# More pairs with seven products in the four output blocks of a hybrid decoder layer, with two input mixes made in the heads' stage

## The chip, the cores and the metric

The kernel runs on one core of a Trainium2 chip, as one program. The metric is the device time of one execution in microseconds (us). A core has five engines with a list of instructions each: TensorE (PE; its weight loads are shown apart, as PEld), VectorE (DVE), ScalarE (ACT), GpSimd (POOL) and SyncE (SP). Each engine goes through its list in order; semaphores make it wait for another engine or a DMA.

## The reference

One decoder layer for 256 tokens of 2048 channels, in float32. The normalised input goes through one wide projection; from it come a latent attention with 16 heads and a gated short convolution. The part that matters here stands behind both:

```python
y_mla = jnp.einsum('bse,ed->bsd', attn, w_o_mla)
...
y_conv = jnp.einsum('bse,ed->bsd', b_gate * conv * jax.nn.silu(z_conv), w_o_conv)
merged = jax.nn.sigmoid(g_mla) * y_mla + jax.nn.sigmoid(g_conv) * y_conv
out = jnp.einsum('bsd,de->bse', merged, w_out)
x = x + _rmsnorm(out, post_norm_g)
```

`g_mla` and `g_conv` are two slices of the wide projection. So four products of 256 x 2048 by 2048 x 2048 are computed in a row: two gates from the normalised input `h`, the attention branch, the convolution branch. The kernel calls them n = 0, 1, 2, 3.

## The kernel before

**Precision.** A float32 product is made of three matmuls: each operand is split into a high and a low half, and high x high, high x low and low x high are added in a bank of PSUM (`product`). For the weights ACT copies the high half (`whi`) and DVE subtracts it to get the low half (`wlo`); both happen in `split_act`. The activations stand split in `x_both` (high in the first 256 columns, low behind them).

**Weights.** All weights are one list of units, `plan`, of 1 MB each (128 x 2048). SP loads them into a ring of three (`raw`); `take(i)` makes sure that unit i is split, and the units behind it are loaded and split ahead. `whi` and `wlo` are rings of five buffers of 1024 columns. A unit is two buffers of each; ACT waits for PE to free the one that it writes.

**Stages.** First come the latents, then 16 heads (`for h in range(H)`), where the matmuls of the wide projection fill in around the attention. Small blocks are transposed on the way: DVE transposes 32 x 32 squares, POOL sends the block to DRAM and brings it back (`turned`: `far`, then `come`). Then come the four products n = 0 to 3, each in two blocks c = 0, 1 of 1024 output columns, and last `w_out` (the name `out`) and the norm. One block adds up eight pairs: pair k covers input features 256 k to 256 k + 255, as a 2 x 2 of blocks of 128 tokens by 128 features, against a 2 x 2 of weight blocks of 128 x 512. A pair is one unit of weights.

**Two kinds of pair.** A plain pair makes the eight products of a 2 x 2 by a 2 x 2, 24 matmuls. A quick pair makes seven (Winograd's form of Strassen's product), 21 matmuls. For that, `split_seven` (L218) forms sums of weight blocks on DVE (`ts`, L224) and splits them too (`th`, `tl`), and `mixed` (L1004) forms differences of input blocks on DVE (`xr` the whole input, `xm` the four differences) and splits them into `mix`. With seven products a block needs eight banks: p1, q5, q6, q7 and p2, q3, q4, d22. `first_sums` combines the first four into the outputs behind the last quick pair of the block; `last_sums` adds the other four at its end.

**Which pairs are quick.** `FAST = (0, 3, 5)` for the two gates (n = 0, 1; in block (0, 0) only 0 and 3), in `fast_block` (L1029). The branches n = 2, 3 have plain pairs only, in `plain_block` (L1077), with four banks a block. In block (0, 0) the order of pairs is 1, 2, 4, 0, 6, 3, 5, 7, and the three mixes are made inside that block, ahead of the second, fourth and sixth pair. The first quick pair there, pair 0, begins with p1, which needs no mix; q5 (from `mix`, `th` and `tl`), q7 and q6 follow, then p2, q3, q4.

**What sets the order.** PE's matmuls are kept in program order. The other engines' instructions are ordered by a scheduler from the program's order and its estimates, unless `keep_in_program_order` pins them. Rings (`tile_pool` with a tag and a number of buffers) decide when an operation may write.

**What the attention block turns into.** While (1, 1) and (2, 0) run, `split_group` splits the attention's output into `x_both`; while (2, 0) and (2, 1) run, the convolution's into `cv_first` and `x_both`. A branch's result multiplies the gate (L1131, L1137) and is added up (L1138); for the last product it is transposed by `turned` and split again (`features`).

Of the kernel before, what the change touches and what calls it, by code (L numbers as in the profile page):

```python
# [11 lines left out]
F32 = mybir.dt.float32  # L12
# [6 lines left out]
P = 128  # L19
S = 256  # L20
# [64 lines left out]
def tile_layer(ctx: ExitStack, tc: tile.TileContext, xw, w0, xb, x, pos, pvec, post_g, wc, wz, wcv, wkr, wqk, wqr, wv, cwr, wd, wo, out):  # L85
# [57 lines left out]
    fast = {(n, c): FAST if n < 2 else () for n in range(4) for c in range(2)}  # L143
    fast[0, 0] = FAST[:2]
    u_d, seven = {}, set()
# [72 lines left out]
    def split_seven(i, t):  # L218
        hi, hi2 = (wpool.tile([P, HALF], F32R, name=f"whi{i}_{j}", tag="whi", bufs=5) for j in range(2))
        lo, lo2 = (wpool.tile([P, HALF], F32R, name=f"wlo{i}_{j}", tag="wlo", bufs=5) for j in range(2))  # L220
# [9 lines left out]
        split_act(hi2[:, :R], lo2[:, :R], t[:, HALF : 3 * R])  # L230
# [4 lines left out]
        return {"b11": b11, "b22": b22, "b21": (hi2[:, :R], lo2[:, :R]), "t1": t1, "t2": t2, "t3": t3, "t4": t4}  # L235
# [86 lines left out]
    x_both = hp.tile([P, KD, 2 * S], F32R, name="x_both")  # L322
    cstack, astack = (main.enter_context(ExitStack()) for _ in range(2))
# [328 lines left out]

    def make(i, j, *more):
        return {"a": group_a, "r": group_r, "v": group_v}[i](j, *more)
# [197 lines left out]
    for h in range(H):  # L852
# [51 lines left out]
        if h == H - 2:  # L904
            score(h + 1)

# [63 lines left out]
    mix = {k: sp.tile([P, 2, 4 * P], F32R, name=f"mix{k}") for k in FAST[::-1]}  # L970
    sums_lo("home")
# [32 lines left out]
    def mixed(k):  # L1004
        tmp = evens(f"xr{k}")
        f = tmp[:, :].rearrange("p (j s) -> p j s", j=2)
        ks = slice(2 * k, 2 * k + 2)
        nc.vector.tensor_tensor(f, x_both[:, ks, :S].bitcast(F32), x_both[:, ks, S:].bitcast(F32), op=ALU.add)
        raw = evens(f"xm{k}")
        a11, a21, a12, a22 = (f[:, j, t * P : (t + 1) * P] for j in range(2) for t in range(2))  # L1010
        m7, m5, m6, m3 = (raw[:, j * P : (j + 1) * P] for j in range(4))
        minus = lambda o, a, b: nc.vector.tensor_tensor(o, a, b, op=ALU.subtract)
        minus(m7, a21, a11)
        minus(m5, a21, a22)
        minus(m6, a11, m5)
        minus(m3, a12, m6)
        split_act(mix[k][:, 0, :], mix[k][:, 1, :], raw[:, :])

    def mix_part(k, j):
        return tuple(mix[k][:, o, j * P : (j + 1) * P] for o in range(2))  # L1020
# [4 lines left out]
    def fast_block(n, c, part, outs, between):  # L1025
        q = {name: bank(f"{name}_{n}{c}") for name in ("p2", "q3", "q4", "d22")}
        q["p1"] = bank(f"p1_{n}{c}", tag="st", bufs=1)
        q["q5"] = bank(f"q5_{n}{c}", tag="o", bufs=1)
        q["q7"], q["q6"] = (bank(f"{name}_{n}{c}", tag="cv", bufs=2) for name in ("q7", "q6"))  # L1029
        order, quick = pair_order[n, c], fast[n, c]  # L1030
        calls = []
# [16 lines left out]
        t_a, t_b = (evens(f"ev{i}_{n}{c}")[:, :] for i in range(2))  # L1048
        (o11, o12), (o21, o22) = outs
        tt = lambda o, a, b, op=ALU.add: nc.vector.tensor_tensor(o, a, b, op=op)  # L1050

        def first_sums():
            nc.scalar.activation(t_a, q["p1"][:, :], AF.Copy)
            tt(t_b, q["q6"][:, :], t_a, ALU.subtract)
            tt(o12, q["q5"][:, :], t_b)
            tt(o21, q["q7"][:, :], t_b)
            tt(o22, q["q5"][:, :], o21)

        def last_sums():
            tt(o11, q["p2"][:, :], t_a)  # L1060
            tt(o12, q["q3"][:, :], o12)
            tt(o21, q["q4"][:, :], o21, ALU.subtract)
            tt(o22, q["d22"][:, :], o22)
# [11 lines left out]
        last_sums()  # L1075

    def plain_block(n, c, part, between):  # L1077
        tags = ("mm",) * 4 if c else ("st", "o", "cv", "cv")
        q = {
            (t, j): bank(f"sq{n}{c}_{t}{j}", tag=tag, bufs={"mm": 4, "cv": 2}.get(tag, 1))  # L1080
            for (t, j), tag in zip(((0, 0), (0, 1), (1, 0), (1, 1)), tags)
        }
        order = pair_order[n, c]
        for at, k in enumerate(order):
            w = take(u_d[n, c, k])
            between(at)
            for (t, j), ps in q.items():
                for i in range(2):
                    b = w({(0, 0): 0, (1, 1): 1, (1, 0): 2, (0, 1): 3}[i, j], R)
                    product(ps[:, :], part(2 * k + i, t), b, at == i == 0, at == PAIRS - 1 and i == 1)  # L1090
        return q
# [6 lines left out]
    for n in range(2):  # L1098
# [4 lines left out]
        for c in range(2):  # L1103

            def between(i):
                if n == c == 0 and i in (1, 3, 5):
                    mixed(FAST[i // 2])
                if n == c == 1 and i in (2, 4, 6):
                    split_group(at_place, at_t, i // 2 - 1)

            outs = [[gate[n][t][:, columns(c, j)] for j in range(2)] for t in range(NT)]
            fast_block(n, c, x_part, outs, between)
# [3 lines left out]
    def between(c, i):  # L1116
# [7 lines left out]
        if (c, i) in ((0, 4), (0, 6), (1, 3), (1, 5)):  # L1124
            split_group(cv_place, cv_t, {(0, 4): 0, (0, 6): 1, (1, 3): 2, (1, 5): 3}[c, i])

    for c in range(2):
        q = plain_block(2, c, x_part, lambda i: between(c, i))
        for (t, j), ps in q.items():
            g = gate[0][t][:, columns(c, j)]  # L1130
            nc.vector.tensor_tensor(g, ps[:, :], g, op=ALU.mult)  # L1131
# [215 lines left out]
```

## Time and profile before

| | us |
|---|---|
| runs: median (lowest to highest) | 1034.54 (1033.6 to 1034.96) |
| the profiled execution | 1034.48 |
| its span, first to last instruction | 1032.7 |
| gate blocks (n = 0, 1), from the first matmul of (0, 0) | 590.2 to 763.6 |
| branch blocks (n = 2, 3) | 763.6 to 937.7 |
| last product and norm | 937.7 to 1032.7 |

The profile is one execution. Its first part has the busy time of each engine and the share of the span; its fourth the chain of work that ended last; its fifth groups of instructions by source line, engine, operation and tile. Every matmul is on line 90 (`matmul`) and every split on L282 (ACT) and L283 (DVE), so groups there are told apart by the tile names. A matmul shows 389 ns from its start to its end, but the next one starts before it ends: busy time and starts are to be read, not the mean. In a timeline a row has the start, the length, the engine, line, operation and tiles, "x2" for two merged instructions, and in brackets the idle time before it and what ended it. A wait put down to "issue" is one for which the profile shows no releaser.

### The profile page before, as it was taken

Reading aid. Unit: us, or ns where it says so; the run is one execution under the profiler, and the core shown is the slowest. Engines: PE = TensorE matmul, PEld = TensorE weight load, DVE = VectorE, ACT = ScalarE, POOL = GpSimd, SP = SyncE. Lnnn points to the kernel's source line nnn. Section 1 sums busy time; section 2 is a strip of 40 time slices with the busy share of each in tenths; the row PEclk is TensorE's granted clock in tenths of the full one; section 3 lists DMA queues with packets and bytes.
Section 4 is the critical chain, followed back from the end, with each engine's and each line's share of the span. In section 5 each row is a group of like instructions: output and inputs, shape, how many; then the busy total and the mean of one; then the engine's idle time right before and its main releaser. Section 6 shows DMA issues by size and latency. Waiting matters only on the chain.

```text
span 1032.7 us, 12827 instructions
## 1 busy us (share of the span) xinstructions
PE 1022.6 (99%) x4651; PEld 851.5 (82%) x4651; DVE 747.4 (72%) x1062; ACT 543.9 (53%) x764; POOL 179.0 (17%) x344
## 2 busy tenths in 40 slices
PE   9999999999999999999999989999999999999998
PEld 7888888888888888888888868888888888888886
DVE  7588777787777777777877798898875554756572
ACT  7665545655456454564555546555654443344451
POOL 4540421104301223112133120000000000214000
PEclk9999999999999999999999989999999999999999
DMA  9775866568665676757676755555555555577852
GB/s 357 276 260 202 279 205 234 213 201 282 218 246 197 220 263 211 273 192 244 229 269 222 260 183 178 226 206 204 204 198 182 193 202 196 197 258 246 344 184 81
DMA packets 44528, 233.26 MB, mean 226 GB/s; under 512 B 7953, under 2 KB 10513, under 8 KB 21553
## 3 DMA queue, kind: packets, MB, share of 16 engines
q1 hardware_dynamic: 32400, 199.67, 54.8%
q0 software_dynamic: 11632, 29.48, 8.8%
q10 hardware_dynamic: 432, 3.29, 0.8%
q8 instruction: 36, 0.59, 0.2%
q14 instruction: 28, 0.22, 0.1%
HBM read 215.66 MB, written 12.58 MB: 221 GB/s over the span
## 4 chain that ended last, share of the span: by engine, by line
PE 97%; DVE 2%; DMA 0%; ACT 0%; issue 0%
PE cv L90 34%; PE sq L90 17%; PE q L90 8%; PE z L90 8%; PE out L90 8%; PE p L90 4%; PE d L90 2%; PE kn L90 2%; PE qa L90 2%; PE qn L90 2%; PE vv L90 2%; PE ckv L90 2%; PE sc L90 1%; PE qr L90 1%; PE o L90 1%; DVE wlo L283 1%
## 5 line engine op out<-in xcount | busy, mean ns | idle before, releaser
L283 DVE TENSOR_TENSOR wlo<-raw,whi 128x1024 fp32r<-128x1024 f32 (+1 forms) x370 | 431.8, 1179 | 202.8 <-ACT whi L282 195.4
L282 ACT ACTIVATE whi<-raw 128x1024 fp32r<-128x1024 f32 (+1 forms) x372 | 373.2, 1021 | 376.0 <-PE cv L90 116.9
L90 PE MATMUL cv<-whi,x_both 128*128 128x512 f32 x1024 | 319.8, 389 | 0.0
L90 PEld LDWEIGHTS cv<-whi,x_both 128*128 128x128 f32 x1024 | 192.3, 188 | 39.4
L90 PE MATMUL cv<-wlo,x_both 128*128 128x512 f32 x512 | 199.6, 390 | 0.0
L90 PE MATMUL sq<-whi,x_both 128*128 128x512 f32 x384 | 118.8, 389 | 0.0
L90 PEld LDWEIGHTS cv<-wlo,x_both 128*128 128x128 f32 x512 | 96.1, 188 | 19.5 <-DVE wlo L283 0.2
L90 PEld LDWEIGHTS sq<-whi,x_both 128*128 128x128 f32 x384 | 72.1, 188 | 15.0
L90 PE MATMUL z<-whi,x_both 128*128 128x512 f32 x256 | 80.0, 389 | 0.0
L90 PE MATMUL out<-whi,x_both 128*128 128x512 f32 x256 | 79.0, 389 | 0.0
L90 PE MATMUL sq<-wlo,x_both 128*128 128x512 f32 x192 | 74.7, 389 | 0.0
L367 POOL DMA_DIRECT2D far<-g x32 | 17.4, 551 | 322.5 <-DVE g L1138 289.9
L367 POOL DMA_DIRECT2D far<-via x64 | 35.2, 556 | 179.2 <-DVE via L359 178.9
L90 PEld LDWEIGHTS out<-whi,x_both 128*128 128x128 f32 x256 | 48.1, 188 | 9.9
L90 PEld LDWEIGHTS z<-whi,x_both 128*128 128x128 f32 x256 | 48.1, 188 | 9.9
L90 PE MATMUL q<-whi,x_both 128*128 128x512 f32 x168 | 55.1, 389 | 0.0
L90 PE MATMUL z<-wlo,x_both 128*128 128x512 f32 x128 | 49.8, 389 | 0.0
L90 PE MATMUL out<-wlo,x_both 128*128 128x512 f32 x128 | 49.8, 389 | 0.0
L90 PE MATMUL p<-whi,x_both 128*128 128x512 f32 x128 | 46.6, 391 | 0.0
L90 PEld LDWEIGHTS sq<-wlo,x_both 128*128 128x128 f32 x192 | 36.0, 188 | 7.4
L367 POOL DMA_DIRECT2D far<-cw x48 | 26.1, 551 | 79.1 <-DVE cw L359 79.1
L90 PE MATMUL sq<-whi,cv_first 128*128 128x512 f32 x128 | 39.7, 389 | 0.0
(253 smaller groups left out, 1433.0 us busy)
## 6 DMA issues: line engine op xcount, KB each, us to landing
raw<-wcv_dram SPq DMA_DIRECT2D x64, 1024.0 KB, 5.9
raw<-wd_dram SPq DMA_DIRECT2D x64, 1024.0 KB, 4.8
raw<-wz_dram SPq DMA_DIRECT2D x16, 1024.0 KB, 4.8
raw<-wo_dram SPq DMA_DIRECT2D x16, 1024.0 KB, 5.0
raw<-wqk_dram SPq DMA_DIRECT2D x8, 1024.0 KB, 6.1
cw<-cwr_dram POOLq DMA_DIRECT2D x24, 256.0 KB, 6.2
raw<-wc_dram SPq DMA_DIRECT2D x4, 1024.0 KB, 10.4
raw<-wv_dram SPq DMA_DIRECT2D x4, 1024.0 KB, 4.8
```

What stands on the lines that cost most here:

```text
L90: return tc.keep_in_program_order(nc.tensor.matmul(*a, **kw))
L282: a = nc.scalar.activation(hi, src, AF.Copy)
L283: b = nc.vector.tensor_tensor(lo, src, hi.bitcast(F32), op=ALU.subtract)
L367: tc.keep_in_program_order(queue.dma_start(out=f[i], in_=m))
```

## The change

Six pairs of the branch blocks become quick: pair 4 in (2, 0), 4 and 6 in (2, 1), 2 and 5 in (3, 0), 2 in (3, 1). `block` replaces `fast_block` and `plain_block`. The pair order of the last three blocks changes so that quick pairs stand late. Where the outputs are not gate tiles (n = 2, 3), the combined sums stand in the ring `ev` and in a tile `more`, and the gate product and the sum read them from there instead of from PSUM. The two groups of four banks change places from block to block.

The mixes of pairs 0 and 3 are made in the heads' stage, at heads 5 and 9, into tiles that exist from the start; pair 5's stays, at the seventh pair of (0, 0), where it is first used in (0, 1). The branches' mixes use the same two tiles again, each made during the block ahead of or at the start of the one that needs it.

A quick unit's single block, b21, gets rings of its own (`ph`, `pl`, 512 columns, two buffers each), where it took half of a wide buffer of `whi` and `wlo`. The space that POOL's DMAs have for descriptors is set to 8192 bytes a partition; the line did not set it before. In `first_sums` two additions change places.

```diff
+    pair_order[2, 1] = [0, 1, 2, 4, 3, 6, 5, 7]
+    pair_order[3, 0] = [0, 1, 3, 4, 2, 6, 5, 7]
+    pair_order[3, 1] = [0, 1, 3, 2, 4, 5, 6, 7]
-    fast = {(n, c): FAST if n < 2 else () for n in range(4) for c in range(2)}
+    fast = {(n, c): FAST for n in range(2) for c in range(2)}
     fast[0, 0] = FAST[:2]
+    fast.update({(2, 0): (4,), (2, 1): (4, 6), (3, 0): (2, 5), (3, 1): (2,)})
...
     def split_seven(i, t):
-        hi, hi2 = (wpool.tile([P, HALF], F32R, name=f"whi{i}_{j}", tag="whi", bufs=5) for j in range(2))
-        lo, lo2 = (wpool.tile([P, HALF], F32R, name=f"wlo{i}_{j}", tag="wlo", bufs=5) for j in range(2))
+        hi, lo = (wpool.tile([P, HALF], F32R, name=f"{o}{i}", tag=o, bufs=5) for o in ("whi", "wlo"))
+        hi2, lo2 = part_hi(f"ph{i}"), part_lo(f"pl{i}")
...
+    def mixed(dst, place, k, rows, raw):
+        xs = [rows(j) for j in range(2)]
+        for j, x in enumerate(xs):
+            area, at = place(2 * k + j)
+            h, l = (area[:, at, o : o + S].bitcast(F32) for o in (0, S))
+            nc.vector.tensor_tensor(x, h, l, op=ALU.add)
+        a11, a21, a12, a22 = (x[:, t * P : (t + 1) * P] for x in xs for t in range(2))
+        m7, m5, m6, m3 = (raw[:, j * P : (j + 1) * P] for j in range(4))
+        minus = lambda o, a, b: nc.vector.tensor_tensor(o, a, b, op=ALU.subtract)
+        minus(m7, a21, a11)
+        minus(m5, a21, a22)
+        minus(m6, a11, m5)
+        minus(m3, a12, m6)
+        split_act(dst[:, 0, :], dst[:, 1, :], raw)
...
+        if h in (HV + 1, 2 * HV + 1):
+            k = FAST[v - 1]
+            mixed(mix[k], lambda k: (x_both, k), k, lambda j: temp("f")[:, :], temp("cw", (P, 512), bufs=2)[:, :])
...
+    def block(n, c, part, mix, between, outs=None):
+        small = [("st", 1), ("o", 1), ("cv", 2), ("cv", 2)]
+        homes = {False: [("mm", 4)] * 4, True: small}
+        sums_at = n < 2 or c == 1
+        q = {}
+        for at, names in ((not sums_at, ("p2", "q3", "q4", "d22")), (sums_at, ("p1", "q5", "q7", "q6"))):
+            for name, (tag, bufs) in zip(names, homes[at]):
+                q[name] = bank(f"{name}_{n}{c}", tag=tag, bufs=bufs)
...
+        if outs is None:
+            more = sp.tile([P, 2 * R], F32, name=f"more_{n}{c}", tag="spare", bufs=1)
+            outs = [[t_a, t_b], [more[:, :R], more[:, R:]]]
...
-                if n == c == 0 and i in (1, 3, 5):
-                    mixed(FAST[i // 2])
+                if n == c == 0 and i == 6:
+                    mixed_in(mix, at_place, FAST[2])
...
+        if (c, i) in ((0, 2), (1, 1)):
+            mixed_in(mix_at, at_place, fast[2, 1][c])
...
-        q = plain_block(2, c, x_part, lambda i: between(c, i))
+        q = block(2, c, x_part, mix_at, lambda i: between(c, i))
...
+        if c == 0 and i in (1, 2):
+            mixed_in(mix_cv, cv_place, fast[3, 0][i - 1])
...
-        q = plain_block(3, c, cv_part, lambda i: features(i - 4) if c and i in (4, 5) else None)
+        q = block(3, c, cv_part, mix_cv, lambda i: between(c, i))
...
-    nc = bacc.Bacc("TRN2", target_bir_lowering=False, num_devices=1)
+    nc = bacc.Bacc("TRN2", target_bir_lowering=False, num_devices=1, dynamic_dma_scratch_size=8192)
```

What the scheduler made of it is shown at two places of DVE's list. A row has the source line, the operation, the tile written and those read, with buffer numbers, and the size. First, the stretch in which DVE prepares pair 0, the first quick pair of block (0, 0). Before, up to its second low half (`tl_1_5676`) and its mix:

```order
L224 TENSOR_TENSOR ts_1_5672<-ts_1_5672,raw_5622 128x512
L1012 TENSOR_TENSOR xm_5634<-xr_5632,xm_5634 128x128
L224 TENSOR_TENSOR ts_0_5758<-raw_5712 128x1024
L283 TENSOR_TENSOR wlo_1024_5719<-raw_5665,whi_1024_5718 128x1024
L1008 TENSOR_TENSOR xr_5722<-x_both 128x512
L283 TENSOR_TENSOR wlo_0_5756<-raw_5712,whi_0_5754 128x1024
L283 TENSOR_TENSOR tl_1_5676<-ts_1_5672,th_1_5674 128x1024
L283 TENSOR_TENSOR mix_5570<-xm_5634,mix_5570 128x512
```

Now, the same pair from its first sum (`ts_0_5686`) to its second low half (`tl_1_5691`):

```order
L228 TENSOR_TENSOR ts_0_5686<-raw_5646 128x1024
L287 TENSOR_TENSOR pl_5685<-raw_5646,ph_5684 128x512
L228 TENSOR_TENSOR ts_1_5687<-ts_0_5686,raw_5646 128x512
L287 TENSOR_TENSOR wlo_0_5730<-raw_5680,whi_0_5729 128x1024
L287 TENSOR_TENSOR wlo_1024_5734<-raw_5680,whi_1024_5733 128x1024
L228 TENSOR_TENSOR ts_1_5687<-ts_1_5687,raw_5646 128x512
L287 TENSOR_TENSOR tl_0_5690<-ts_0_5686,th_0_5688 128x1024
L287 TENSOR_TENSOR pl_5763<-raw_5727,ph_5762 128x512
L287 TENSOR_TENSOR tl_1_5691<-ts_1_5687,th_1_5689 128x1024
```

The operations on `xr`, `xm` and `mix` are gone from this stretch, and so is the next quick pair's first sum (`ts_0_5758`), which stood ahead of the second low half.

Second, the branch block (2, 1) on DVE. Before, at its start, with the gate products of block (2, 0) (`g<-sq`) and plain units only:

```order
L1131 TENSOR_TENSOR g_1_5573<-sq_11_6915,g_1_5573 128x512
L283 TENSOR_TENSOR wlo_1024_7220<-raw_7171,whi_1024_7219 128x1024
L283 TENSOR_TENSOR wlo_0_7250<-raw_7213,whi_0_7249 128x1024
L283 TENSOR_TENSOR wlo_1024_7254<-raw_7213,whi_1024_7253 128x1024
L283 TENSOR_TENSOR wlo_0_7284<-raw_7247,whi_0_7283 128x1024
L283 TENSOR_TENSOR wlo_1024_7288<-raw_7247,whi_1024_7287 128x1024
L283 TENSOR_TENSOR wlo_0_7318<-raw_7281,whi_0_7317 128x1024
L283 TENSOR_TENSOR wlo_1024_7322<-raw_7281,whi_1024_7321 128x1024
L283 TENSOR_TENSOR x_both<-cv_f,x_both 128x4x128 x2
```

Now, up to the second low half (`tl_1_7352`) of pair 4, the fourth pair of that block:

```order
L228 TENSOR_TENSOR ts_1_7348<-ts_0_7347,raw_7297 128x512
L287 TENSOR_TENSOR wlo_1024_7304<-raw_7263,whi_1024_7303 128x1024
L666 TENSOR_TENSOR xm_7308<-xr_7307,xm_7308 128x128
L287 TENSOR_TENSOR tl_0_7351<-ts_0_7347,th_0_7349 128x1024
L287 TENSOR_TENSOR wlo_7344<-raw_7297,whi_7343 128x1024
L228 TENSOR_TENSOR ts_1_7348<-ts_1_7348,raw_7297 128x512
L666 TENSOR_TENSOR xm_7308<-xr_7307,xm_7308 128x128
L287 TENSOR_TENSOR wlo_0_7391<-raw_7341,whi_0_7390 128x1024
L287 TENSOR_TENSOR wlo_1024_7395<-raw_7341,whi_1024_7394 128x1024
L287 TENSOR_TENSOR x_both<-cv_f,x_both 128x4x128 x2
L228 TENSOR_TENSOR ts_0_7429<-raw_7388 128x1024
L287 TENSOR_TENSOR tl_1_7352<-ts_1_7348,th_1_7350 128x1024
```

Behind the two parts of the unit that follows (`wlo_0_7391`, `wlo_1024_7395`), a split of the convolution's output and the first sum of the next quick pair (`ts_0_7429`) DVE comes to `tl_1_7352`.

80 lines of the change are left out of this document (28 added, 52 removed).

## The prediction

> **What bounds the kernel now.** The profile's page comes first: the span, the busy time of TensorE (PE), and the chain of work that ended last.
>
> ```profile
> span 1032.7 us, 12827 instructions
> PE 1022.6 (99%) x4651; PEld 851.5 (82%) x4651; DVE 747.4 (72%) x1062; ACT 543.9 (53%) x764; POOL 179.0 (17%) x344
> PE 97%; DVE 2%; DMA 0%; ACT 0%; issue 0%
> ```
>
> PE is the bound, so only two things can save time: fewer matmuls, and fewer waits of PE. The waits of PE between 560 and 765 us (engine, line, releaser: total, times, longest) are two, one behind the other:
>
> ```profile
> PE q L90 <- issue: 2.3, 1, 2.3
> PE q L90 <- DVE mix L283: 1.4, 1, 1.4
> ```
>
> The chain in order of time (start, length, what) gives the price of a matmul where nothing waits:
>
> ```profile
> 763.60 174.08 PE sq L90 x768
> 937.68 87.05 PE out L90 x384
> ```
>
> 174.08 / 768 and 87.05 / 384 are both 0.2267 us per matmul; the 389 ns that a group shows as the mean of one is its latency, with neighbours overlapping. I charge 0.2267 throughout.
>
> The waits lie in the first gate block, at its first quick pair (pair 0, fourth in the order). PE's timeline there, and the two operations that write pair 0's mix:
>
> ```profile
> 607.04 0.39 PE L90 MATMUL p<-whi,x_both 128*128 128x512 f32 x1
> 609.74 0.77 PE L90 MATMUL q<-th,mix 128*128 128x512 f32 x1 [2.31 <-issue]
> 610.30 0.63 PE L90 MATMUL q<-tl,mix 128*128 128x512 f32 x1
> 612.31 1.22 PE L90 MATMUL q<-th,mix 128*128 128x512 f32 x2 [1.38 <-DVE mix L283]
> ...
> 616.55 0.40 PE L90 MATMUL q<-whi,mix 128*128 128x512 f32 x1
> ```
>
> ```profile
> 609.03 0.61 ACT L282 ACTIVATE mix<-xm 128x512 fp32r<-128x512 f32 x1
> 611.56 0.69 DVE L283 TENSOR_TENSOR mix<-xm,mix 128x512 fp32r<-128x512 f32 x1
> ```
>
> The first product with the mix starts 0.10 us after ACT wrote its high half (609.64), although the page calls that wait "issue". The third starts 0.06 us after DVE wrote its low half (612.25). From 607.04 to 616.55 stand 13 matmul steps: 13 x 0.2267 = 2.95 us of work in 9.51 us. So this place loses 6.56 us, of which 3.69 us are the two waits and the rest a slower PE behind them. The table by stretches shows that as the granted clock (third-last column: 1.00 before, 0.66 in it):
>
> ```profile
> 590.00:607.00 17.00, 17.00 (x78) 14.11 (x77) 16.96 (x26) 7.25 (x9) 5.50 (x10) 1.00 0.52 181
> 607.00:617.00 10.00, 6.31 (x16) 4.22 (x16) 9.49 (x15) 4.47 (x7) 0.00 (x0) 0.66 0.59 219
> 617.00:763.60 146.60, 146.60 (x648) 121.45 (x647) 128.01 (x145) 86.84 (x101) 0.00 (x0) 1.00 0.57 200
> 763.60:807.00 43.40, 43.40 (x193) 35.93 (x193) 25.08 (x26) 20.38 (x25) 0.00 (x0) 1.00 0.55 194
> 807.00:850.60 43.60, 43.60 (x194) 36.13 (x193) 23.78 (x24) 18.25 (x21) 0.00 (x0) 1.00 0.54 195
> 850.60:894.00 43.40, 43.40 (x194) 35.93 (x193) 21.96 (x22) 15.97 (x17) 0.00 (x0) 1.00 0.55 192
> 894.00:937.70 43.70, 43.70 (x194) 36.23 (x193) 28.46 (x33) 18.35 (x21) 10.92 (x20) 1.00 0.70 243
> ```
>
> Columns: stretch, length, busy PE, PEld, DVE, ACT, POOL, clock, DMA share, GB/s. The other gate blocks (617 on) run PE without a gap while DVE is busy 128.0 of 146.6 us (87%). The four branch blocks have DVE at only 50 to 65%: that is the room which the change spends.
>
> **Part 1: six more quick pairs.** Each has seven products instead of eight, three matmuls each: 6 x 3 = 18 matmuls fewer, on the engine that sets the end. 18 x 0.2267 = **4.08 us** off.
>
> **Part 2: two mixes made in the heads' stage.** The mix of pair 0 is then ready some 350 us before its use, so both waits go. What is late next at that place is DVE's own work for the pair. Intervals on DVE come from neighbours' starts:
>
> ```profile
> 609.29 1.23 DVE L283 TENSOR_TENSOR wlo<-raw,whi 128x1024 fp32r<-128x1024 f32 x1
> 610.42 1.23 DVE L283 TENSOR_TENSOR tl<-ts,th 128x1024 fp32r<-128x1024 f32 x1
> ...
> 612.16 0.69 DVE L224 TENSOR_TENSOR ts<-ts,raw 128x512 f32<-128x512 f32 x1
> 612.76 0.50 DVE L1012 TENSOR_TENSOR xm<-xr 128x128 f32<-128x128 f32 x2
> 564.70 0.42 DVE L435 TENSOR_TENSOR f<-o,half 128x256 f32<-128x256 f32 x1
> 565.03 0.69 DVE L824 TENSOR_TENSOR mv<-mv,mv 128x512 f32<-128x512 f32 x1
> ```
>
> That is 1.14 us for 1024 columns, 0.60 for 512, 0.33 for 256; 128 columns are 0.50 - 0.29 = 0.20. DVE is full ahead of the quick pair (16.96 of the 17 us up to 607); these rows are the anchor:
>
> ```profile
> 596.93 2.36 DVE L283 TENSOR_TENSOR wlo<-raw,whi 128x1024 fp32r<-128x1024 f32 x2
> 599.20 0.71 DVE L359 STREAM_TRANSPOSE mv<-cv_f 128x512 f32<-128x512 f32 x1
> 599.83 0.66 DVE L1008 TENSOR_TENSOR xr<-x_both 128x512 f32<-128x512 f32 x1
> ```
>
> In the new order DVE goes from the transpose straight to pair 0's sums. From 599.83: sum 1.14, part 0.60, sum 0.60, the next unit's two halves 2.28, sum 0.60, first low half 1.14 gives 606.2; another part 0.60 and the second low half 1.14 give 607.9. PE wants the first at 607.27 + 0.23 = 607.5 and the second in q6's second product, 7 steps after 607.27, at 608.9. Both are in time, by 1.3 and 1.0 us, so I take **6.56 us** off, clock loss included.
>
> The price is two mixes on DVE at heads 5 and 9, each 2 x 0.33 + 4 x 0.20 + 0.60 = 2.1 us, and one ACT copy of 0.61. They stand inside a head's softmax, and delay its transpose by about 2 us:
>
> ```profile
> 255.30 0.57 DVE L359 STREAM_TRANSPOSE via<-p 128x384 f32<-128x384 f32 x1
> 255.70 2.17 POOL L367 DMA_DIRECT2D far<-mv  x4
> 257.86 1.63 POOL L367 DMA_DIRECT2D far<-via  x3
> ```
>
> POOL sends the transposed block only at 257.86, behind another that it has begun at 255.70; 255.87 + 2.1 = 257.97 is 0.1 us too late. What it sends is used one head later. Cost nothing; uncovered it would be at most 2 x 2.1 us.
>
> **Part 3: what the new quick pairs cost DVE.** A plain unit costs it 2 x 1.14 = 2.28 us; a quick one 1.14 + 0.60 + 2 x 1.14 for low halves and 1.14 + 2 x 0.60 for sums, 6.36: 4.08 more. A block's combining sums are eight of 0.60, 4.8. A mix is 2.1. With the busy times above: block (2,0) 25.1 + 4.1 + 2.1 + 4.8 = 36.1 of 42.8 us (189 matmuls); (2,1) 23.8 + 8.2 + 2.1 + 4.8 = 38.9 of 42.2 (186); (3,0) 22.0 + 8.2 + 4.2 + 4.8 = 39.2 of 42.2; (3,1) 28.5 + 4.1 + 4.8 = 37.4 of 42.8. That is 84, 92, 93 and 87%, against the 87% at which the gate blocks hold PE without a gap.
>
> So averages allow it, and the tightest pair must be checked. By DVE's new list that is pair 4 in (2,1). From the end of p2 of (2,0), which comes 18 matmuls (4.08 us) before that block ends, to the second low half of pair 4 stand 11 operations of 1.14, 13 of 0.60, two of 0.33 and four of 0.20: 21.8 us, so it is ready 17.7 us into (2,1). PE wants it after three pairs and seven steps, (72 + 7) x 0.2267 = 17.9. The margin is 0.2 us. The same sum for the other new pairs leaves 1 us or more. A unit's lists 5% longer than I count would cost 1.1 us here. I charge **0.2 us**, bounds 0 and 1.1, nearer to 0 because the same kind of row gave these intervals.
>
> **Part 4: edits with one answer.** The rings for single parts give back one buffer of each wide ring per quick pair; PE waits for none between 617 and 763 us, so nothing is gained. A block now takes all eight banks; the four that the next needs first are freed by the first sums, 0.6 (ACT) + 4 x 0.60 = 3.0 us, beneath the 5.44 us of the plain pair that follows at least: nothing, and without that cover 3 us a block. ACT writes the high half wherever DVE writes a low one, so it gets no more than DVE's 52 us, in blocks where it is busy 73 of 174: nothing. The lists of SP and POOL keep their order.
>
> At the end of (3,1) the combining sums delay the last transposed piece from 7.9 us after the block's end (945.57) to 12.9.
>
> ```profile
> 944.95 0.71 DVE L359 STREAM_TRANSPOSE g<-g 128x512 f32<-128x512 f32 x1
> 956.18 0.55 POOL L371 DMA_DIRECT2D g<-far  x1 [1.51 <-DMA far<-g]
> g<-far POOLq DMA_DIRECT2D x8, 256.0 KB, 6.2
> ```
>
> The last return goes out at 18.5 + 5.0 = 23.5 us and lands 6.2 later, 29.7. PE first reads any returned piece after six units, 6 x 5.44 = 32.6 us, and this one later still: covered by 2.9 us. The halved descriptor space of POOL's DMAs is not visible in this trace; bounds 0 and the 2 us that one of its transfers takes to issue. I take 0, as nothing in the trace shows POOL short of it.
>
> **The sum.** The profiled execution took 1034.48 us (span 1032.7, 1.78 around it), 0.06 below the median of 1034.54. 1034.48 - 4.08 - 6.56 + 0.2 = 1024.04; on the median's scale **1024.1 us**.
>
> **Rivals.** A: pair 0's second low half comes late after all (its cover is 1.0 us of a chain of ten operations). A wait of 1 us would cost 1 us, and, if the clock falls as it did here, up to 12 matmuls at 0.42 instead of 0.23 (the 10 from 612.31 to 616.55 took 4.24), 2.3 more: 1025.1 to 1027.4. For it: DVE is full from 590 on. Against: the sum above.
>
> [...]
>
> B: the branch blocks run DVE too full (92 and 93% in the middle two). Four of the six new pairs then wait 1.1 us each: 4.4, giving 1028.5. For it: the margin of 0.2 us. Against: the gate blocks at 87%.
>
> C, the slower side: at the new pairs ACT and DVE wait in line for ring buffers that PE has yet to free, so PE meets a wait like that of 607 us, with its slow clock, 6.56 us each. Two give 1037.2, slower than before; four give 1050.3. It decides from the second such wait on. Against: from 617 to 763 us ten quick pairs pass without one.
>
> D: the mix is not what held pair 0, and only part 1 and its 1.38 us wait come off: 1034.5 - 4.1 - 1.4 = 1029.0. Against: the start 0.10 us after ACT's mix.
>
> **Chances.** Forecast 0.74, A 0.10, B 0.09, C 0.03, D 0.04. Differences below 0.2% (2 us) can't be told from none here. All but C are faster than 1032.5; for tails of B and D I leave 0.02 as no change: faster 0.95, same 0.02, slower 0.03. The range starts 0.9 below the forecast's floor of 1023.8 (the runs spread that far below their median) and reaches through A towards B: 1022.9 to 1027.6.
>
> **What would show it.** Right: 4633 matmuls; no PE wait at pair 0 and a clock of 1.00 there; branch blocks of 42.8, 42.2, 42.2 and 42.8 us. Wrong: a wait at q6 of pair 0 for DVE (A); waits at tl in (2,1) and (3,0) (B); waits of 2 us with a lowered clock there (C); a wait at q5 of pair 0 for th (D). A wait of PE in the heads' stage would show that part 2 has a price.

## The result and the profile after

The changed kernel takes 1024.09 us (median of 4 runs, 1023.74 to 1024.30) against 1034.07 us of the kernel before (4 runs): ratio 0.9902, 95% interval 0.9885 to 0.9919. The profiled execution took 1023.97 us, with a span of 1022.2.

The page of the kernel after, its span, busy times and chain:

```profile
span 1022.2 us, 12864 instructions
PE 1016.1 (99%) x4633; PEld 846.9 (83%) x4633; DVE 796.2 (78%) x1155; ACT 557.5 (55%) x784; POOL 180.3 (18%) x344
PE 99%; DMA 0%; ACT 0%; DVE 0%; issue 0%
```

There are 18 matmuls fewer (4651 - 4633), DVE works 48.8 us more, and the chain is PE alone: DVE's 2% of before is gone from it.

PE's timeline at pair 0 of block (0, 0), and DVE's two low halves for it:

```profile
606.87 0.39 PE L90 MATMUL p<-whi,x_both 128*128 128x512 f32 x1
607.09 0.39 PE L90 MATMUL q<-th,mix 128*128 128x512 f32 x1
607.32 0.39 PE L90 MATMUL q<-tl,mix 128*128 128x512 f32 x1
...
608.68 0.39 PE L90 MATMUL q<-tl,mix 128*128 128x512 f32 x1
```

```profile
604.84 1.22 DVE L287 TENSOR_TENSOR tl<-ts,th 128x1024 fp32r<-128x1024 f32 x1
...
606.58 1.22 DVE L287 TENSOR_TENSOR tl<-ts,th 128x1024 fp32r<-128x1024 f32 x1
```

No gap is left: q5 starts one step (0.22 us) behind p1. DVE has the first low half ready at 604.84 + 1.22 = 606.06, 1.3 us before PE takes it (607.32), and the second at 607.80, 0.9 us before 608.68.

The table by stretches of the kernel after (columns as before: stretch, length, busy PE, PEld, DVE, ACT, POOL, clock, DMA share, GB/s):

```profile
607.00:617.00 10.00, 10.00 (x46) 8.29 (x45) 8.96 (x9) 4.94 (x6) 0.00 (x0) 1.00 0.72 270
756.60:799.50 42.90, 42.90 (x191) 35.53 (x190) 32.98 (x40) 23.36 (x29) 0.00 (x0) 1.00 0.55 197
799.50:841.70 42.20, 42.20 (x188) 34.91 (x187) 38.35 (x50) 22.48 (x27) 0.00 (x0) 1.00 0.53 199
841.70:883.90 42.20, 42.20 (x188) 34.95 (x187) 38.26 (x52) 21.60 (x25) 0.00 (x0) 1.00 0.58 205
883.90:926.80 42.90, 42.90 (x190) 35.20 (x189) 37.04 (x46) 19.54 (x23) 10.95 (x20) 1.00 0.67 238
```

The clock between 607 and 617 us is 1.00, where it was 0.66, and PE is busy through the four branch blocks. DVE fills 91% of the middle two.

**A finer measure than the whole time.** The first matmul of the gate blocks starts at another time in each execution (589.46 to 590.90 us in the profiles of this study, in no order of the edits), because what comes ahead of it jitters. From there to the first matmul of the last product the same work stands in every kernel. Its two rows, of before and of after:

```profile
590.23 0.39 PE L90 MATMUL p<-whi,x_both 128*128 128x512 f32 x1
937.52 0.39 PE L90 MATMUL out<-whi,x_both 128*128 128x512 f32 x1
```

```profile
590.05 0.39 PE L90 MATMUL p<-whi,x_both 128*128 128x512 f32 x1
926.99 0.39 PE L90 MATMUL out<-whi,x_both 128*128 128x512 f32 x1
```

347.29 us before, 336.94 after: 10.35 less. What follows is the same in both (937.52 to 1032.7 and 926.99 to 1022.2, 95.2 us each). The stage is that of the one profiled execution of each kernel; the whole times are medians, and each ratio is to the runs of the kernel before that were made beside it:

| kernel | stage, us | against after | whole time, median (range), us | ratio to before (95%) |
|---|---|---|---|---|
| before | 347.29 | +10.35 | 1034.07 (1033.55 to 1034.96) | |
| after | 336.94 | | 1024.09 (1023.74 to 1024.30) | 0.9902 (0.9885 to 0.9919) |
| mixes only | 340.72 | +3.78 | 1027.65 (1027.30 to 1027.91) | 0.9938 (0.9923 to 0.9953) |
| quick pairs only | 344.96 | +8.02 | 1031.04 (1030.17 to 1031.40) | 0.9967 (0.9955 to 0.9978) |
| descriptor space only | 347.35 | +10.41 | 1034.41 (1033.66 to 1035.33) | 1.0000 (0.9991 to 1.0009) |
| old rings | 337.65 | +0.71 | 1024.55 (1024.30 to 1024.81) | 0.9908 (0.9894 to 0.9923) |
| pair 6 in (2, 0) too | 336.40 | -0.54 | 1023.56 (1023.26 to 1023.79) | 0.9893 (0.9880 to 0.9907) |
| pair 5 in (3, 1) too | 338.15 | +1.21 | 1025.51 (1024.74 to 1026.87) | 0.9916 (0.9902 to 0.9929) |
| first sum written twice | 340.96 | +4.02 | 1028.18 (one run) | |
| first sum written five times | 348.56 | +11.62 | 1035.30 (one run) | |
| later pair in (3, 1) | 336.65 | -0.29 | 1023.30 (1022.93 to 1023.70) | 0.9893 (0.9879 to 0.9908) |
| later, and pair 6 in (2, 0) | 335.96 | -0.98 | 1023.12 (1022.55 to 1023.73) | 0.9892 (0.9877 to 0.9906) |
| the same, and pair 5 in (3, 1) | 335.28 | -1.66 | 1022.33 (1022.20 to 1023.16) | 0.9886 (0.9871 to 0.9900) |
| before, pair 0 later | 352.47 | +15.53 | 1038.87 (1038.66 to 1040.25) | 1.0047 (1.0030 to 1.0064) |

### The profile page after: what moved, and what is told of

Same layout as the page of the kernel before. It is cut to its first block, busy times and chain, and to the rows that moved or that the text cites. A ratio compares the mean times of both kernels' runs of the same rounds, so it can differ in the third digit from the quotient of the medians.

```text
span 1022.2 us, 12864 instructions
## 1 busy us (share of the span) xinstructions
PE 1016.1 (99%) x4633; PEld 846.9 (83%) x4633; DVE 796.2 (78%) x1155; ACT 557.5 (55%) x784; POOL 180.3 (18%) x344
## 4 chain that ended last, share of the span: by engine, by line
PE 99%; DMA 0%; ACT 0%; DVE 0%; issue 0%
PE cv L90 34%; PE q L90 18%; PE p L90 9%; PE z L90 9%; PE out L90 9%; PE d L90 6%; PE qa L90 2%; PE kn L90 2%; PE qn L90 2%; PE vv L90 2%; PE ckv L90 2%; PE sc L90 1%; PE qr L90 1%; PE o L90 1%; PE kr L90 0%; DMA raw<-w_dram 0%
## 5 line engine op out<-in xcount | busy, mean ns | idle before, releaser
L286 ACT ACTIVATE whi<-raw 128x1024 fp32r<-128x1024 f32 (+1 forms) x355 | 360.5, 1032 | 335.3 <-PE cv L90 112.9
L287 DVE TENSOR_TENSOR wlo<-raw,whi 128x1024 fp32r<-128x1024 f32 (+1 forms) x353 | 417.0, 1192 | 150.8 <-ACT whi L286 143.7
L90 PE MATMUL q<-whi,x_both 128*128 128x512 f32 x328 | 107.7, 389 | 0.0
L90 PEld LDWEIGHTS q<-whi,x_both 128*128 128x128 f32 x328 | 61.6, 188 | 12.9
L90 PE MATMUL p<-whi,x_both 128*128 128x512 f32 x194 | 68.8, 389 | 0.0
L90 PE MATMUL q<-wlo,x_both 128*128 128x512 f32 x164 | 63.8, 389 | 0.0
L90 PE MATMUL d<-whi,x_both 128*128 128x512 f32 x164 | 57.1, 389 | 0.0
L286 ACT ACTIVATE th<-ts 128x1024 fp32r<-128x1024 f32 x34 | 35.8, 1053 | 14.7 <-DVE ts L228 11.1
L90 PEld LDWEIGHTS p<-whi,x_both 128*128 128x128 f32 x194 | 36.4, 188 | 7.6
L287 DVE TENSOR_TENSOR tl<-ts,th 128x1024 fp32r<-128x1024 f32 x34 | 41.4, 1216 | 1.4 <-ACT th L286 1.3
```

Of the source, the lines that this page charges most:

```text
L90: return tc.keep_in_program_order(nc.tensor.matmul(*a, **kw))
L286: a = nc.scalar.activation(hi, src, AF.Copy)
L287: b = nc.vector.tensor_tensor(lo, src, hi.bitcast(F32), op=ALU.subtract)
```

## The experiments

The theory is that of the prediction: the late mix and the slow clock behind it cost 6.56 us at pair 0, the six quick pairs bring their 18 matmuls, and nothing else has a price of over half a us. The rivals are those of the prediction.

**The mixes without the quick pairs.** The branch blocks go back to the plain pairs of before:

```diff
-    fast.update({(2, 0): (4,), (2, 1): (4, 6), (3, 0): (2, 5), (3, 1): (2,)})
+    fast.update({(n, c): () for n in (2, 3) for c in range(2)})
...
-        q = block(2, c, x_part, mix_at, lambda i: between(c, i))
+        q = plain_block(2, c, x_part, lambda i: between(c, i))
```

> The changed kernel with the four branch blocks computed by plain pairs, as before; the two mixes are made in the heads' stage, and the rings and the smaller descriptor space are those of the change. Theory (the mix held pair 0): 1034.1 - 6.56 = 1027.5 us, no wait of PE at pair 0, clock 1.00 between 607 and 617 us. Rival D (something else held pair 0, and only the 1.4 us wait for the mix comes off): 1032.7 us. Rival (the quick pairs themselves bring less than 3.9 us, the place at pair 0 more): below 1026 us.

It took 1027.65 us. The stretch at pair 0, in this kernel's table:

```profile
607.00:617.00 10.00, 10.00 (x46) 8.29 (x45) 8.77 (x10) 5.33 (x6) 0.00 (x0) 1.00 0.68 274
```

PE has no gap there and the clock is 1.00. The stage is 347.29 - 340.72 = 6.57 us shorter than before, against 6.56 expected, and rival D is out. (Both figures are read from the same execution of before, so they show that nothing of its loss at pair 0 is left; the whole times differ by 6.95 from the 1034.60 us of the runs of before made beside it.) What after has beyond this kernel is 3.78 us: the quick pairs' part.

**The quick pairs without the early mixes.** The mixes are made in block (0, 0) again:

```diff
-        if h in (HV + 1, 2 * HV + 1):
-            k = FAST[v - 1]
-            mixed(mix[k], ...)
...
-                if n == c == 0 and i == 6:
-                    mixed_in(mix, at_place, FAST[2])
+                if n == c == 0 and i in (1, 3, 5):
+                    mixed_in(mix, at_place, FAST[i // 2])
```

> The changed kernel with the three mixes of the gate blocks made inside the first gate block again, at its places 1, 3 and 5; the six new quick pairs and all else stay. Theory: the wait at pair 0 and its slow clock are back, 6.6 us or, as the last parts of the mix now stand up to 1.8 us further back in DVE's list, up to 8.4: 1030.6 to 1032.4 us with 4633 matmuls. Rival D (the mix isn't what held pair 0): at most 1.4 us more than the changed kernel, 1025.5 us.

It took 1031.04 us, and the stage is 8.02 us longer than after. PE's timeline at pair 0, and ACT's copy of the mix:

```profile
606.27 0.39 PE L90 MATMUL p<-whi,x_both 128*128 128x512 f32 x1
609.05 0.47 PE L90 MATMUL q<-th,mix 128*128 128x512 f32 x1 [2.39 <-issue]
...
612.27 1.22 PE L90 MATMUL q<-th,mix 128*128 128x512 f32 x2 [2.53 <-DVE mix L287]
```

```profile
608.34 0.61 ACT L286 ACTIVATE mix<-xm 128x512 fp32r<-128x512 f32 x1
```

PE goes on 0.10 us after ACT's copy (608.95), the same distance as in the kernel before, though the copy stands at another time. So ACT's copy is the releaser that the profile calls "issue". The two waits are 4.92 us by the idle times in brackets. These count from the end of the matmul before (0.39 us behind its start), while without a wait the next one starts 0.23 us behind that start; so each wait costs PE 0.16 us more than its bracket, and the two cost 5.2 us. The slow clock lasts until 618.33 (last section), and the 6.06 us of matmuls in it, from 612.27 on, run at a granted clock of 0.50 and cost half of that, 3.0 us more. (Together that is 0.2 us more than 8.02, as this kernel does not have the wait of 0.27 us that after has in (3, 1).)

**The descriptor space alone.** The kernel before with one argument added:

```diff
-    nc = bacc.Bacc("TRN2", target_bir_lowering=False, num_devices=1)
+    nc = bacc.Bacc("TRN2", target_bir_lowering=False, num_devices=1, dynamic_dma_scratch_size=8192)
```

> The kernel before with the descriptor space of the DMAs halved, and nothing else. Theory (that space has no price): 1034.1 us, within 0.3, and POOL's transfers issue as before (2.2 us for four). Rival (POOL has to wait for descriptors): up to 2 us slower, 1036 us, with longer issues at POOL in the heads' stage.

The ratio is 1.0000 (0.9991 to 1.0009) and the stage 347.35 us: nothing, as predicted. One of POOL's transfers still takes 0.55 us to issue (`far<-via`: a median of 551 ns in both traces). (The kernel before leaves the size to its default, and no run shows that 8192 bytes are half of it.)

**The single parts back in the wide rings.**

```diff
-        hi, lo = (wpool.tile([P, HALF], F32R, name=f"{o}{i}", tag=o, bufs=5) for o in ("whi", "wlo"))
-        hi2, lo2 = part_hi(f"ph{i}"), part_lo(f"pl{i}")
+        hi, hi2 = (wpool.tile([P, HALF], F32R, name=f"whi{i}_{j}", tag="whi", bufs=5) for j in range(2))
+        lo, lo2 = (wpool.tile([P, HALF], F32R, name=f"wlo{i}_{j}", tag="wlo", bufs=5) for j in range(2))
```

> The changed kernel with the single block's two parts of a quick unit back in the wide rings of five, which they shared before; all else stays. Theory (the rings give nothing, as PE waits for none of them): 1024.1 us, within 0.4. Rival (with two quick pairs near each other the wide rings run out, ACT waits for a buffer that PE has yet to free, and PE for ACT): a wait of 1 to 2 us at two to four of the new quick pairs, 1026 to 1032 us.

It took 1024.55 us; the intervals of the two ratios overlap. The stage is 0.71 us longer, and the trace has one wait for it, in block (3, 1):

```profile
903.03 0.50 PE L90 MATMUL q<-tl,mix 128*128 128x512 f32 x1 [0.71 <-DVE tl L287]
```

So the rings are worth at most 0.7 us, in the tightest block. The edit also moves DVE's order there, so how much of the 0.7 is buffers and how much order stays open.

**One more quick pair where DVE has room.**

```diff
-    fast.update({(2, 0): (4,), (2, 1): (4, 6), ...})
+    fast.update({(2, 0): (4, 6), (2, 1): (4, 6), ...})
...
-        if (c, i) in ((0, 2), (1, 1)):
-            mixed_in(mix_at, at_place, fast[2, 1][c])
+        if c == 0 and i in (2, 3):
+            mixed_in(mix_at, at_place, fast[2, 1][i - 2])
```

> The changed kernel with one more quick pair: pair 6 of block (2,0), whose mix is made in (2,0) at place 3 instead of in (2,1). Theory (where DVE has room, a quick pair brings its three matmuls): DVE in (2,0) goes from 33.0 us to 33.0 + 4.1 + 2.1 = 39.2 of 42.2 us (93%), in (2,1) from 38.4 to 36.3; 4630 matmuls, 0.68 us less, 1023.4 us, ratio 0.9896 against the kernel before. Rival B (DVE too full at 93%): a wait of 1 us or more at pair 6 of (2,0) or in (2,1), 1024.4 us or more.

1023.56 us; the stage is 0.54 us shorter than after, 0.68 being the three matmuls. DVE's busy time in (2, 0) came to 38.95 us of 42.2, the 39.2 expected, and PE waited for nothing there. The missing 0.14 lies in (3, 1), where the short wait of after is a little longer.

**One more where it has not.**

```diff
-    fast.update({..., (3, 1): (2,)})
+    fast.update({..., (3, 1): (2, 5)})
```

> The changed kernel with one more quick pair: pair 5 of block (3,1), with the mix that (3,0) has made. DVE there would go from 37.0 to 41.1 us of 42.2 (97%), behind a place that already waits 0.27 us. Theory (a quick pair brings its three matmuls, but each us by which DVE is late is a us of PE): waits of 1 to 3 us in (3,1) against 0.68 us saved, 1024.4 to 1026.4 us. Rival (averages up to 97% still hide DVE): 1023.4 us. Rival C (the waits bring the slow clock with them): 1027 us or more.

1025.51 us, and 1.21 us more in the stage of its profiled execution, the fastest of five. PE's two waits, and what ACT did ahead of them:

```profile
912.87 0.51 PE L90 MATMUL q<-th,mix 128*128 128x512 f32 x1 [0.85 <-ACT th L286]
914.13 0.51 PE L90 MATMUL q<-tl,mix 128*128 128x512 f32 x1 [0.76 <-DVE tl L287]
```

```profile
909.38 2.01 ACT L286 ACTIVATE whi<-raw 128x1024 fp32r<-128x1024 f32 x2 [1.93 <-PE d L90]
911.30 0.58 ACT L1071 ACTIVATE ev<-p 128x512 f32<-128x512 f32 x1
911.78 1.04 ACT L286 ACTIVATE th<-ts 128x1024 fp32r<-128x1024 f32 x1
```

ACT was idle for 1.93 us, until PE freed the buffers of the next unit's two copies; the copy that PE needed (`th`, done at 912.82) stood behind these in ACT's list. DVE began the low half for the second wait at 912.85: its list, too, has the two low halves of the next unit first, until 912.84. DVE is busy 90% of this block (39.34 of 43.8 us), though from 905.60 to 914.07 it pauses for only 0.2 us. So the quick pair was late because the next unit's work stood ahead of its own in both lists; over the whole block no engine was full.

The clock stayed at 1.00 in this execution. Two of the other four took 1026.34 and 1026.87 us, with a mean clock of 0.998 over the whole run where the rest have 0.999 or 1.000; 3.41 us at a clock of 0.50, the shortest slow piece of the last section, would lower the mean over 1025 us by 0.0017. So rival C may have come in these two, at one slow piece each; they left no trace, so this is not shown.

**How long a gap lowers the clock.** DVE writes the first sum of pair 0 once or four times more:

```diff
+        for _ in range(1 if i == u_d[0, 0, 0] else 0):
+            plus(two(ta[:, :]), two(t[:, :HALF]), t[:, 3 * R :].unsqueeze(1).to_broadcast([P, 2, R]))
         plus(tb[:, :R], ta[:, :R], t[:, R:HALF])
```

> The changed kernel with the first sum of pair 0 of block (0,0) written twice by DVE (the same values, 1.14 us more); it delays the pair's second low half, which PE would then want at 608.7 us and get at about 611.2: one gap of about 2.5 us, and no second one behind it. Rival A's price by the trace (a gap of 2.3 us lowers the clock): 2.5 + up to 2.9 us, 1029 us, clock below 0.9 between 607 and 617. [...]

> The same first sum written five times (4.6 us more of DVE work): by DVE's list PE waits about 3.9 us for the first high half and 2.1 us for the low one behind it. By the trace's rule the clock falls behind the first gap: 6.0 us of waits and 3 to 4 us of slow matmuls, 1033 to 1034 us. [...]

With one sum more it took 1028.18 us (stage +4.02), with four 1035.30 (stage +11.62). PE's waits in the first, then the longer one of two in the second:

```profile
609.15 0.50 PE L90 MATMUL q<-th,mix 128*128 128x512 f32 x1 [0.27 <-ACT th L288]
611.47 0.57 PE L90 MATMUL q<-tl,mix 128*128 128x512 f32 x1 [1.81 <-DVE tl L289]
```

```profile
613.94 0.77 PE L90 MATMUL q<-th,mix 128*128 128x512 f32 x1 [6.96 <-issue]
```

Behind a gap of 1.81 us, with one of 0.27 ahead of it, the granted clock was 0.50 from 612.00 to 615.00 (0.83 on average between 607 and 617 us): 2.08 us of waits cost 4.02. The slow clock came as the price by the trace had it, and 1029 us was 0.8 too much. In the second kernel my list of DVE gave 3.9 us for the first wait; it was 6.96. ACT's timeline there has the reason:

```profile
611.84 1.06 ACT L288 ACTIVATE whi<-raw 128x1024 fp32r<-128x1024 f32 x1 [5.12 <-DMA raw<-wd_dram]
612.80 1.04 ACT L288 ACTIVATE th<-ts 128x1024 fp32r<-128x1024 f32 x1
```

The copy that PE needs (`th`, done at 613.84) stood behind one that waited 5.12 us for a weight load.

**The small wait that is left.** In the kernel after, PE has one wait between 590 and 930 us, by the weight loads' waits (total, times, longest), in (3, 1); DVE's timeline ahead of it:

```profile
PEld p L90 <- DVE wlo L287: 0.4, 1, 0.4
```

```profile
882.00 1.22 DVE L228 TENSOR_TENSOR ts<-raw 128x1024 f32<-128x1024 f32 x1 [0.89 <-DMA raw<-wd_dram]
...
886.75 1.22 DVE L287 TENSOR_TENSOR tl<-ts,th 128x1024 fp32r<-128x1024 f32 x1
...
889.09 1.21 DVE L287 TENSOR_TENSOR wlo<-raw,whi 128x1024 fp32r<-128x1024 f32 x1
```

The low half at 889.09 is that of the block's second unit, done at 890.30. PE's row for it, and the piece of the chain that it belongs to:

```profile
890.36 0.50 PE L90 MATMUL p<-wlo,cv_first 128*128 128x512 f32 x1
```

```profile
889.45 1.63 PE p L90 x6
```

PE takes it 0.06 us after it is done, and the six matmuls take 1.63 us where six without a wait take 1.36: 0.27 us late. Ahead of it in DVE's list stand the sums and parts of the quick pair, the block's fourth, which PE needs only some 10 us later, and for whose load DVE even waits 0.89 us. The experiment puts that quick pair one place later:

```diff
-    pair_order[3, 1] = [0, 1, 3, 2, 4, 5, 6, 7]
+    pair_order[3, 1] = [0, 1, 3, 4, 2, 5, 6, 7]
```

> The changed kernel with the quick pair of block (3,1) one place later (pairs in the order 0, 1, 3, 4, 2, 5, 6, 7). DVE's list then has the quick unit's sums and parts (1.14 + 0.60 + 0.60 + 1.14 = 3.5 us, and the 0.89 us for which DVE waited for that unit's load) behind the second half of the block's second unit instead of ahead of it. Theory (this order makes the 0.27 us wait of PE at 890 us): the wait is gone, span 0.3 us shorter, 1023.8 us. Rival (the block's combining sums alone are what is late there): the wait stays, 1024.1 us.

1023.30 us; the stage is 0.29 us shorter than after, and no wait of PE is left in it. The same low half in this kernel, and PE's matmul with it:

```profile
885.56 1.22 DVE L287 TENSOR_TENSOR wlo<-raw,whi 128x1024 fp32r<-128x1024 f32 x1
```

```profile
889.61 0.39 PE L90 MATMUL p<-wlo,cv_first 128*128 128x512 f32 x1
```

It is ready at 886.78, 2.8 us early. The order was the cause. (The whole time fell by more, 0.79 us. In the two profiled executions the gate blocks start 0.59 us apart, at 589.46 and 590.05, which no edit explains.)

**Both together, and a second quick pair in (3, 1).** First the later order with the additional pair 6 in (2, 0); then with pair 5 as the last but one of (3, 1) as well, whose diff this is:

```diff
-    pair_order[3, 1] = [0, 1, 3, 2, 4, 5, 6, 7]
+    pair_order[3, 1] = [0, 1, 3, 4, 2, 6, 5, 7]
...
-    fast.update({(2, 0): (4,), ..., (3, 1): (2,)})
+    fast.update({(2, 0): (4, 6), ..., (3, 1): (2, 5)})
```

> The changed kernel with the later quick pair in (3,1) and the additional quick pair 6 in (2,0). Theory: both effects add, 0.68 + 0.3 us, 1023.1 us with 4630 matmuls and no wait of PE between 560 and 930 us. Rival (the wait only moves to another unit of (3,1)): 1023.5 us.

> As the kernel with the later quick pair and the additional pair in (2,0), and a second quick pair in (3,1), pair 5, as its last but one (order 0, 1, 3, 4, 2, 6, 5, 7). Theory (DVE was late in the run with two quick pairs in (3,1) because both stood in its first six units, behind the combining sums of (3,0); towards its end DVE has idle time, 9 us of it after 905 us): 4627 matmuls, another 0.68 us off, 1022.4 us. Rival B (a mean load of 97% can't be hidden wherever the pairs stand): waits of 1 to 2 us as with the earlier order, 1024 to 1025 us.

The stage is 0.98 and 1.66 us shorter than after, against 0.95 and 1.63 expected, and the whole times are 1023.12 and 1022.33 us. Block (3, 1) of the second:

```profile
884.00:926.20 42.20, 42.20 (x188) 34.92 (x187) 40.35 (x50) 21.96 (x26) 10.95 (x20) 1.00 0.68 249
```

DVE is busy 40.35 of 42.2 us, 96%, and PE does not wait. With the same two quick pairs at earlier places it waited 1.6 us (0.85 + 0.76), though DVE was busy only 90% of the block. This last version is the fastest measured: 1.66 us less than after in the stage, while the intervals of the two whole-time ratios still overlap.

**Another way around the late mix.** The kernel before with one line changed, so that the mixes have one unit more of time:

```diff
-    pair_order[0, 0] = [1, 2, 4, 0, 6, 3, 5, 7]
+    pair_order[0, 0] = [1, 2, 4, 6, 0, 5, 3, 7]
```

> The kernel before with another order of the pairs in block (0,0) alone: 1, 2, 4, 6, 0, 5, 3, 7, so that pair 0 is wanted one unit (5.44 us) later and pair 3 one unit later; the mixes are still made in that block. Theory (the mix is late by 2.3 us and the second high half by 1.4 more, less than one unit): no gap over 1 us at pair 0, the clock stays at 1.00, 6 us less than before, 1028 us. Rival (DVE is full from 590 us on, 16.96 of 17 us, so it takes the added unit's halves first and pair 0 is late again): a wait of 1 to 3 us and the slow clock, 1031 to 1034 us.

It took 1038.87 us, slower than before: ratio 1.0047 (1.0030 to 1.0064). The two stretches, at pair 0 and at the start of (0, 1), and PE's waits in the second:

```profile
607.00:617.00 10.00, 10.00 (x46) 8.29 (x45) 9.64 (x14) 6.70 (x9) 0.00 (x0) 1.00 0.67 242
632.00:642.00 10.00, 1.50 (x5) 0.80 (x5) 9.23 (x13) 4.10 (x6) 0.00 (x0) 0.73 0.31 123
```

```profile
633.76 0.50 PE L90 MATMUL p<-whi,x_both 128*128 128x512 f32 x1 [1.53 <-ACT ev L1053]
641.68 0.79 PE L90 MATMUL q<-th,mix 128*128 128x512 f32 x1 [6.96 <-DVE g L1050]
```

The wait at pair 0 is gone, as the theory had it. But pair 3, now the last but one, leaves the block's first sums one plain pair (5.44 us) before (0, 1) wants the same banks for p1 and q5. The first of them is ACT's copy of p1 (`ev<-p`). It stands behind a weight copy that waits 3.49 us for PE, and behind the copy of a mix:

```profile
631.64 1.06 ACT L282 ACTIVATE whi<-raw 128x1024 fp32r<-128x1024 f32 x1 [3.49 <-PE d L90]
...
633.13 0.58 ACT L1053 ACTIVATE ev<-p 128x512 f32<-128x512 f32 x1
```

DVE begins its sums at 635.62, behind a low half, a weight sum and the mix's low half, and takes more of such work between them until 639.15. So PE waits 8.5 us for two banks, and the clock is 0.51 from 637 to 647 us. Neither my theory nor the rival had this.

## Why the prediction was right, point by point

**The sum.** 1024.1 us was predicted, 1024.09 measured. That the whole times agree to 0.01 us is luck: the forecast took 10.44 us (4.08 + 6.56 - 0.2) from a median of 1034.54, while the runs of before beside the result have 1034.07, 9.98 more than after, and the runs of after spread over 0.56 us. The fairer test is the stage: 10.44 us were to go, and 10.35 went.

**Part 2, the mixes** (6.56 us). Shown by the kernel with the mixes alone: 6.57. Of the two margins, 1.3 us is as predicted and the other 0.9 instead of 1.0. The split of the 6.56 us was off: with 0.16 us more for each wait than its bracket says, the waits are 4.0 us and not 3.69, and the slow clock is the other 2.5. The total is that of one execution (last section). The mixes' price in the heads' stage was put at nothing. No wait of PE came into the heads' stage: from 60 to 590 us PE is busy 530.00 of 530.00 us in both profiles. The gate blocks start at 590.05 us, where they started at 590.23, but that start jitters by more.

**Part 1, the quick pairs** (4.08 us). Shown: 3.78, which is 18 matmuls less one wait of 0.27 (3.81), to the 0.06 us by which before and the descriptor space alone differ in the stage.

**Part 3, DVE.** The busy times in the middle blocks were to be 38.9 and 39.2 us, and are 38.35 and 38.26; block (2, 0) has 32.98 where I wrote 36.1, as its last four sums (2.4 us) run behind its end. The 0.2 us charged has the right size at the wrong place. It was charged to pair 4 of (2, 1), and the sum for that pair was wrong: I counted seven steps of PE behind three pairs and left out p1's three. The rows of DVE and PE for it:

```profile
816.49 1.22 DVE L287 TENSOR_TENSOR tl<-ts,th 128x1024 fp32r<-128x1024 f32 x1
```

```profile
799.53 0.39 PE L90 MATMUL p<-whi,x_both 128*128 128x512 f32 x1
...
818.12 0.39 PE L90 MATMUL q<-tl,mix 128*128 128x512 f32 x1
```

PE takes the low half 818.12 - 799.53 = 18.6 us into the block, not at 17.9. DVE has it at 817.71, 18.2 us in, not at 17.7. Two errors of opposite sign left 0.4 us, and no wait. "The same sum for the other new pairs leaves 1 us or more" was the step that failed. It went through the quick pairs' own low halves only, and the wait fell on the plain unit ahead of a quick one, in (3, 1), because DVE's list has the quick unit's sums first.

**Part 4.** The descriptor space costs nothing, shown. (Its bound of 2 us was misread: 2.17 us is the issue of four transfers, and one takes 0.55.) The rings were put at nothing, and taking them back costs up to 0.7 us in (3, 1). The eight banks cost nothing here; but "without that cover 3 us a block" was too low: the kernel with pair 0 later shows 8.5 us of waits and a clock of 0.51 behind them where the sums have one plain pair as cover and stand behind other work. The cover alone does not decide: in (3, 0) of the kernel after one plain pair follows the last quick one too, and PE does not wait. The tail is unchanged, 95.2 us both times.

**Rivals.** A did not come, and its price is now measured: 2.08 us of waits cost 4.02, where I had given a wait of 1 us up to 2.3 of slow clock. B is wrong as put. At 91, 92 and even 96% of DVE's time PE need not wait; in the two places taken apart in (3, 1), at 890 us in after and at 912 us with pair 5 added, an order in a list is the cause. C did not come in the changed kernel. Its mechanism, a copy that waits in ACT's list for buffers that PE has yet to free, is the one seen with pair 5 added in (3, 1), at 0.85 and 0.76 us instead of 6.56, and with the clock at 1.00 in the execution that was profiled. D is refuted.

## What to carry to other kernels

A gap of PE is to be priced with the slow clock behind it, where one comes: 2.08 us of waits were worth 4.02 with the first sum written twice, while 1.61 us (0.85 and 0.76) with pair 5 added in (3, 1) left the clock at 1.00. Moving the late operand's work to a stage where its engine has room (DVE was busy 401.7 of the 530 us from 60 to 590 in the kernel before) took back all of the 6.56 us at pair 0. Before adding work to an engine that hides behind PE, go through its list in order and ask of every entry, not only of the new ones, when PE wants what stands behind it; the busy share (86 and 90% with a wait, 91, 92 and 96% without) did not tell. When a product is moved later in a block, look at what frees the banks for the next block: a wait more than twice as long as the one removed came up there.

## What the runs showed of the hardware

At pair 0 the granted clock went from 1.00 to 0.50 and back, once in each of four executions. Its mean in the half microsecond around its fall and its end tells both times, as the half microseconds ahead of the fall and behind the end have 1.00, and those between 0.50. The rows of before, of the kernel with one sum more, of the one with four more, and of the one with the quick pairs only:

```profile
609.00:609.50 0.50, 0.00 (x0) 0.00 (x0) 0.50 (x2) 0.50 (x2) 0.00 (x0) 0.98 0.89 377
616.00:616.50 0.50, 0.50 (x3) 0.40 (x2) 0.50 (x1) 0.05 (x1) 0.00 (x0) 0.70 0.00 0
```

```profile
611.50:612.00 0.50, 0.50 (x2) 0.42 (x3) 0.00 (x0) 0.00 (x0) 0.00 (x0) 0.75 0.98 410
615.00:615.50 0.50, 0.50 (x4) 0.40 (x3) 0.50 (x2) 0.44 (x1) 0.00 (x0) 0.84 0.00 0
```

```profile
611.00:611.50 0.50, 0.00 (x0) 0.00 (x0) 0.00 (x0) 0.00 (x0) 0.00 (x0) 0.67 0.16 66
621.00:621.50 0.50, 0.50 (x3) 0.40 (x2) 0.00 (x0) 0.00 (x0) 0.00 (x0) 0.59 0.93 213
```

```profile
611.50:612.00 0.50, 0.00 (x0) 0.00 (x0) 0.50 (x2) 0.29 (x1) 0.00 (x0) 0.50 0.93 360
618.00:618.50 0.50, 0.50 (x3) 0.43 (x2) 0.50 (x1) 0.28 (x1) 0.00 (x0) 0.67 1.12 475
```

Before: a mean of 0.98 puts the fall 4% of the half microsecond ahead of 609.50, at 609.48; a mean of 0.70 puts the end at 616.30. That is 6.82 us. In the same way 611.75 to 615.16 is 3.41 us, 611.17 to 621.41 is 10.24, and 611.50 to 618.33 is 6.83. The shortest of the four is 3.41 us; the others are two and three times as long.

The table has PE's waits at pair 0, each by the matmul starts on its two sides, beside the times of the clock:

| kernel | first wait | second wait | clock falls | clock is back |
|---|---|---|---|---|
| before | 607.04 to 609.74 | 610.30 to 612.31 | 609.48 | 616.30 |
| first sum written twice | 608.49 to 609.15 | 609.15 to 611.47 | 611.75 | 615.16 |
| first sum written five times | 606.59 to 613.94 | 613.94 to 615.94 | 611.17 | 621.41 |
| quick pairs only | 606.27 to 609.05 | 609.36 to 612.27 | 611.50 | 618.33 |

The length of a wait alone does not tell whether the clock falls in it. In the kernel before it fell in the first wait, 2.44 us behind the last start ahead of it. With the quick pairs only, the first wait was 0.08 us longer, start to start, and the clock stayed at 1.00 through it and fell in the second, 2.14 us behind the last start. With the first sum written twice it fell 0.28 us after PE had gone on. With pair 5 added in (3, 1), waits of 0.85 and 0.76 us left it at 1.00. Nor was the way back the same: from the end of the second wait, behind which PE worked without a break, the slow clock lasted another 3.99, 3.69, 5.47 and 6.06 us, in the order of the table. What decides the two times is not shown by these runs.

The mean clock differs between executions of one kernel as well. Of the runs of the kernel before that were made beside the experiments, those with a mean clock of 0.998 took 1033.4 to 1034.8 us, those with 0.995 or 0.996 took 1035.2 to 1035.9. The 6.56 us are the price in the profiled execution, with 0.997. That pair 0 has another price in the others is not shown, as only one execution left a trace.
